# Squares of four RMS norms: from GpSimd to ScalarE and VectorE, and later in the order

## The chip, the core and the metric

The kernel runs on one core of a Trainium2 chip. The metric is the device time of one execution in microseconds, the median of several runs. The engines are TensorE (PE in the profile), VectorE (DVE), ScalarE (ACT), GpSimd (POOL) and SyncE (SP), which issues nearly all DMAs.

## What is computed

Two layers of an encoder trunk on 256 tokens of 1024 features, in float32. Before each of four sublayers stands an RMS norm, and one at the end:

```python
def rms_norm(x, g):
    xf = x.astype(jnp.float32)
    y = xf * lax.rsqrt(jnp.mean(xf * xf, axis=-1, keepdims=True) + RMS_EPS)
    return (y * g.astype(jnp.float32)).astype(x.dtype)
...
    for layer in range(DEPTH):                       # DEPTH = 2
        xn = rms_norm(x, norm_mix[layer])
        if layer % 2 == 0:                           # neighbourhood + latent attention
            x = x + even_mixer(xn, ...)
        else:                                        # dilated sliding windows
            x = x + odd_mixer(xn, ...)
        x = x + sq_relu_mlp(rms_norm(x, norm_mlp[layer]), mlp_w1[layer], mlp_w2[layer])
    return rms_norm(x, norm_final)
```

The change concerns the mean of `xf * xf` in the first four norms.

## The kernel before

The tokens `x` lie transposed in SBUF: 128 partitions of features, eight tiles of features, 256 tokens each. A float32 product runs as three passes on TensorE over operands that are split in two parts of lower precision: high x high, low x high, high x low. The high part is a copy by ScalarE, the low part a subtraction by VectorE. For the weights these are `whi` (L167) and `wlo` (L168), made from `raw`, which SyncE's DMAs fill ahead of time (four buffers of `raw`, three of the split parts). A piece of weights is split in four parts of 128x512 or less. For the tokens they are `xh` (L207, tokens times gain) and `xl` (L208).

The factor 1 / rms is not put onto the tokens. The products take the tokens times the gain, and the factor follows where their results go. So the sum of squares is needed some time after the products begin. Squares of two tiles of features at a time are added into `squares`, 128 x 512, whose halves are added at the end (`add_squares`, L214 to L218). TensorE sums over the partitions by a product with a constant: `columns` (L224) or `inverse_row` (L244). GpSimd takes the power -1/2 (L232, L198).

There are five stages, and the four that the change touches begin like this:

- The start: for each of eight tiles of features `xh`, `xl` and a piece of `w_c` are made, and six products of 416 columns follow (the low-rank inputs of the latent attention). Then come the values of the neighbourhood attention (`v_steps`, products of 512 columns), for two tiles of tokens, in two halves of features each. Here the order on TensorE, ScalarE and VectorE is the order of the code (`manual_schedule`).
- Handovers 1, 2 and 3 (`hand_over`): the last products of a stage end pair by pair; for each pair of tiles VectorE adds the residual (L282, L284), then `xh` and `xl` are made, with a raised priority. Handover 1 leads into the first MLP, 2 into the odd layer, 3 into the last MLP. In an MLP the first piece of `w1` takes 48 products of 256 columns (`up(0)`), in the odd layer the first values take 48 products of 384 columns.

Outside of the manual part a scheduler sets the order on each engine, by priorities and its own estimates. An engine works off its instructions in that order.

Of the kernel before, what the change touches and what calls it, by code (L numbers as in the profile page):

```python
"""Two layers of a hybrid encoder trunk (neighbourhood + latent attention, then dilated
attention, each with a squared-ReLU MLP) on one core.

The float32 products of the projections run as three passes over operands split into two
float32r parts each (12 + 12 bits): high*high + low*high + high*low.
"""
# [12 lines left out]
AF = mybir.ActivationFunctionType  # L19
# [4 lines left out]
P = 128  # L24
D = 1024
KT = D // P
T = 256
# [17 lines left out]
def trunk(ctx, tc, a, out):  # L45
# [9 lines left out]
    def scratch(shape, name):  # L55
        """A rotating [P, 512] float32 tile, seen in another shape."""
        n = int(np.prod(shape))
        v = work.tile([P, 512], F32, tag="scratch", name=name, bufs=12)[:, :n]
        if len(shape) == 2:
            v = v.rearrange("p (a b) -> p a b", b=shape[1])  # L60
        return v
# [12 lines left out]
    # the array's clock rises with work: keep it busy until the first operands are there  # L74
# [21 lines left out]
    # ---------------------------------------------------------------- weights  # L96
# [61 lines left out]
    def weight():  # L158
        """The next piece of the weights, as its two parts; those after it are on their way."""
        j = state["used"]  # L160
        prefetch(j + 1, j + 1)
        prefetch(j + LOAD_AHEAD, j + SPLIT_AHEAD)
        state["used"] = j + 1
        return parts.pop(j)[1:]
# [10 lines left out]
    def two_heads(o, hi, lo, ts):  # L175
        """Scores of two heads, in the two halves of the rows, in turns."""
        for n, (y, z) in enumerate(((hi, hi), (hi, lo), (lo, hi))):
            for j in range(2):
                pb = slice(64 * j, 64 * j + 64)
                nc.tensor.matmul(o[j], y[pb, 0, ts], z[pb, 1, :], start=n == 0, stop=n == 2)  # L180

    def weave(main, side, lead=0):
        """Issue two lists of steps, the second spread evenly over the first from lead on."""
        done = 0
        for i, step in enumerate(main):
            step()
            while done < len(side) and done * (len(main) - lead) < (i + 1 - lead) * len(side):
                side[done]()
                done += 1
# [4 lines left out]
    # ------------------------------------------------------------------ norms  # L194
    # The products take the tokens times the gain alone; 1 / rms follows where their results go.
# [5 lines left out]
    def two(z):  # L201
        return z.rearrange("p (f n) -> p f n", f=2)

    def prepare(k, n, xT):
        """The gain of norm n on a tile of features, and its two parts: steps."""
        hi, lo, gk = xT[0][:, k, :], xT[1][:, k, :], gains[:, n * KT + k:n * KT + k + 1]
        return (lambda: nc.scalar.activation(hi, x[:, k, :], AF.Copy, scale=gk),  # L207
                lambda: nc.vector.scalar_tensor_tensor(lo, x[:, k, :], gk, hi.bitcast(F32), ALU.mult, ALU.subtract))  # L208

    def add_squares(b, s):  # L210
        """Squares of two tiles of features onto their sum; the last leaves one of all."""
        v = x[:, 2 * b:2 * b + 2, :]
        q = scratch([2, T], "q") if b else two(s)
        nc.gpsimd.tensor_tensor(q, v, v, op=ALU.mult)  # L214
        if b:
            nc.gpsimd.tensor_tensor(two(s), two(s), q, op=ALU.add)
        if b == 3:
            nc.gpsimd.tensor_tensor(s[:, 0:T], s[:, 0:T], s[:, T:2 * T], op=ALU.add)  # L218

    def columns(s):  # L220
        """Mean square + EPS of the tokens, as a column for each tile of them."""
        pr = bank("w")
        for t in range(NT):
            nc.tensor.matmul(pr[:, t:t + 1], s[:, tok(t)], mean[:, 0:1], start=True, stop=True)  # L224
        ms = work.tile([P, NT], F32, tag="ms", name="ms")
        nc.vector.tensor_scalar(ms, pr[:, 0:NT], EPS, None, ALU.add)
        return ms

    def rstd(s):
        """1 / rms of the tokens, as columns."""  # L230
        r = work.tile([P, NT], F32, tag="rstd", name="rstd")
        nc.gpsimd.tensor_tensor(r, columns(s), mhalf.broadcast_to([P, NT]), op=ALU.pow)  # L232
        return r

    def inverse_columns(s):
        """1 / mean square of the tokens, as columns."""
        inv = columns(s)
        nc.vector.reciprocal(inv, inv)
        return inv

    def inverse_row(s):
        """1 / mean square of the tokens, as a row that is the same for all partitions."""
# [12 lines left out]
    def as_row(dg):  # L255
        """Columns, given as diagonals, as a row that is the same for all partitions."""
        pr = bank("w")
        for t in range(NT):
            nc.tensor.matmul(pr[:, tok(t)], mean, dg[t], start=True, stop=True)
        return pr[:, 0:T]  # L260
# [11 lines left out]
    def hand_over(accs, last, n, scale=None):  # L272
        """The residual, in pairs of tiles of features, while the products of the next pair run."""
        xT = half_tile(act, "xh", 2), half_tile(act, "xl", 2)
        s = sum_tile()
        for b in range(4):
# [10 lines left out]
            add_squares(b, s)  # L287
# [5 lines left out]
    def onto(accs, w, c, v, m, first, last, fbs):  # L293
        """Products of a tile of features, [feature, token], for some of the eight tiles of sums."""
# [7 lines left out]
    def out_steps(accs, mixed, wo, k):  # L302
        """A tile of features of the output projection, in two steps."""
# [6 lines left out]
    def out_last(accs, mixed, wo):  # L310
        """The last two tiles of features, by pairs of tiles of sums."""
# [7 lines left out]
    def mlp(mp, xT, invert, tail, make_down, beside=lambda j: None):  # L319
        """The first product and the second but for its last pieces of weights: returns what  # L320
        these take."""
        hs = {}

        def up(j):
            w = weight()
            pu = bank("w")
            # the last features of the first piece come later than the others
# [13 lines left out]

        for j in range(3):
            up(j)
        inv = invert()
# [11 lines left out]
    def mlp_between(mp, xT, s):  # L356
# [5 lines left out]
        accs, hs, inv, w = mlp(mp, xT, lambda: inverse_row(s), range(14, 16), down)  # L362
# [8 lines left out]
    def finish(mp, xT, s):  # L371
        """The last MLP and the final norm, [token, feature]."""
# [17 lines left out]
        def tokens_first(j):  # L390
            """Transpose the tokens back, a part at a time."""
# [7 lines left out]
        accs, hs, inv, w = mlp(mp, xT, lambda: inverse_columns(s), tail, down, tokens_first)  # L399
# [22 lines left out]
        # the last tile piece by piece, so that little is left after the last product  # L422
# [22 lines left out]
    # ============================================================== even layer  # L445
    def even(ep):
# [17 lines left out]
        def rope(dst, src, n, cos, sin, half):  # L464
            """dst, src [P, n, 2*half]; cos, sin [P, 2*half], the sine signed."""
# [8 lines left out]
        # low-rank inputs of the latent attention, its shared rotary key, and the  # L474
        # values of the neighbourhood attention
# [53 lines left out]
        with tc.manual_schedule(engines={ENG.PE, ENG.Activation, ENG.DVE}):  # L529
            for k in range(KT):  # L530
# [8 lines left out]
                if k % 2:  # L539
                    add_squares(k // 2, s)  # L540
# [3 lines left out]
        with tc.issue_after(ins[0]), tc.issue_after(ins[1]):  # L544
            with tc.manual_schedule(engines={ENG.PE, ENG.Activation, ENG.DVE}):
                v0, v1 = v_steps(0), v_steps(1)
                v0(range(4))
                small_loads()
                r = rstd(s)
                dg = [diagonal(r, t) for t in range(NT)]  # L550
                v1(range(4))
# [6 lines left out]
        # queries and keys of the neighbourhood attention, [head dim of two heads, token]  # L558
# [21 lines left out]
        # latent attention: queries, keys, values  # L580
# [56 lines left out]
        # both attentions: two heads of one tile of queries at a time, in three steps  # L637
# [10 lines left out]
        def scores(n):  # L648
            kind, t, hp = items[n]
            load_bias(n + 2)  # L650
            # the two heads of the neighbourhood attention lie in different row tiles: a bank each
# [47 lines left out]
        def attention():  # L699
            """Steps for all items, each a step behind the one before, the first with time to go by."""  # L700
# [20 lines left out]
        # the steps of the projections with their time on the tensor engine, and between them,  # L721
        # spread evenly after the first, those of the attention
# [21 lines left out]
    # =============================================================== odd layer  # L744
    def odd(op, xT, s):
# [7 lines left out]
        # keys of the two strided groups of a head, block diagonal for each class of tokens  # L753
# [13 lines left out]
        def value_steps(d):  # L767
            """Steps for the values of two heads in the three groups, [token, feature]."""
# [23 lines left out]
        def qk_steps(d):  # L792
            """Steps for the queries and keys of two heads, [feature, token]: of the first group,
            both heads; then by head those of the other two."""
# [85 lines left out]
        run_all(v0[0::2] + v0[1::2])  # L880
# [40 lines left out]
def _order():  # L921
    """Tokens by class modulo 4, then 16; the strided groups attend within a class."""
# [25 lines left out]
def _layout(i):  # L948
# [10 lines left out]
    # queries and keys of two heads: the first group's, then by head those of the other two  # L959
# [8 lines left out]
    # bias of [query, key], where the key is in the query's window, else a filling  # L968
# [33 lines left out]
```

## Time and profile before

| | |
|---|---|
| Median of 3 runs | 787.64 us (786.34 to 788.21) |
| Span of the profiled execution, first to last instruction | 787.1 us; the profile gives no other time of its own for it |
| TensorE busy | 766.1 us, 97% of the span |
| VectorE, ScalarE, GpSimd busy | 516.8, 500.7, 47.9 us |
| Mean granted TensorE clock | 0.990 |
| DMA | 129.14 MB, mean 164 GB/s |

A row of a timeline gives the start, the duration, the engine, the line, the operation with the tiles it writes and reads, how many such instructions are merged into it, and in brackets the engine's idle time ahead of it with what ended it. Matmuls overlap: a product lasts 0.28 us in the record while the next starts 0.12 us after it, so a pace is read from starts. A row of a window gives the stretch and its length, the busy time of each engine, the granted clock and the DMA share.

### The profile page before, as it was taken

How to read it: one execution, taken by the hardware profiler on the slowest of the kernel's cores; microseconds unless marked ns; L12 is line 12 of the kernel's file. 1: busy time of each engine (PE TensorE's matmuls, PEld its weight loads, DVE VectorE, ACT ScalarE, POOL GpSimd, SP SyncE). 2: the span in 40 equal slices, each digit the busy share in tenths (PEclk: the TensorE clock that was granted, in tenths of full speed). 3: DMA queues.
4: the chain of work that ended last, by engine and by line, in shares of the span. 5: the costliest groups of instructions: out<-in, count | busy, mean ns of one | idle time of the engine just before them, and what ended most of it. 6: DMA issues, size and time to landing. Idle time of an engine off the chain costs nothing. (4 is left out here: it accounts for less than half of the span.)

```text
span 787.1 us, 14625 instructions
## 1 busy us (share of the span) xinstructions
PE 766.1 (97%) x5898; PEld 723.9 (92%) x5898; DVE 516.8 (66%) x1012; ACT 500.7 (64%) x1062; POOL 47.9 (6%) x54
## 2 busy tenths in 40 slices
PE   7999998999999999899999999999998999999996
PEld 5898898999999999799999999999997999999996
DVE  7778859665555548777676767676749555546554
ACT  6578964444545444588989889889854545545451
POOL 5100004000000002300000000000004000000000
PEclk9999999999999999899999999999999999999999
DMA  8754223544545544444535434535453544555511
GB/s 297 271 202 149 108 107 107 202 174 163 212 167 185 184 168 162 161 138 144 174 126 183 149 134 162 166 117 200 147 197 114 214 164 172 199 184 191 166 50 53
DMA packets 22819, 129.14 MB, mean 164 GB/s; under 512 B 2912, under 2 KB 5472, under 8 KB 9824
## 3 DMA queue, kind: packets, MB, share of 16 engines
q1 hardware_dynamic: 22464, 127.94, 46.2%
q8 instruction: 46, 0.75, 0.4%
q10 hardware_dynamic: 288, 0.28, 0.1%
q14 instruction: 21, 0.17, 0.1%
HBM read 127.16 MB, written 1.05 MB: 163 GB/s over the span
## 5 line engine op out<-in xcount | busy, mean ns | idle before, releaser
L168 DVE TENSOR_TENSOR wlo<-raw,whi 128x512 fp32r<-128x512 f32 (+3 forms) x488 | 314.0, 677 | 165.8 <-ACT whi L167 164.8
L167 ACT CAST whi<-raw 128x512 fp32r<-128x512 f32 (+3 forms) x488 | 268.9, 600 | 220.4 <-issue 178.0
L172 PE MATMUL w<-xl,whi 128*128 128x256 f32 x528 | 150.9, 286 | 5.8 <-DVE xl L208 5.8
L173 PE MATMUL w<-xh,wlo 128*128 128x256 f32 x528 | 149.6, 283 | 0.0
L171 PE MATMUL w<-xh,whi 128*128 128x256 f32 x528 | 149.4, 283 | 0.0
L171 PE MATMUL acc<-xh,whi 128*128 128x256 f32 x432 | 125.3, 290 | 0.0
L173 PE MATMUL acc<-xh,wlo 128*128 128x256 f32 x432 | 121.8, 282 | 0.0
L172 PE MATMUL acc<-xl,whi 128*128 128x256 f32 x432 | 121.7, 282 | 0.0
L172 PEld LDWEIGHTS w<-xl,whi 128*128 128x128 f32 x528 | 99.9, 189 | 8.0 <-DVE xl L208 7.5
L171 PEld LDWEIGHTS w<-xh,whi 128*128 128x128 f32 x528 | 100.4, 190 | 0.5
L173 PEld LDWEIGHTS w<-xh,wlo 128*128 128x128 f32 x528 | 100.3, 190 | 0.0
L171 PEld LDWEIGHTS acc<-xh,whi 128*128 128x128 f32 x432 | 81.4, 188 | 2.4 <-issue 1.4
L172 PEld LDWEIGHTS acc<-xl,whi 128*128 128x128 f32 x432 | 81.5, 189 | 0.0
L173 PEld LDWEIGHTS acc<-xh,wlo 128*128 128x128 f32 x432 | 81.2, 188 | 0.0
L171 PE MATMUL acc<-hh,whi 128*128 128x256 f32 x256 | 72.6, 284 | 0.0
L172 PE MATMUL acc<-hl,whi 128*128 128x256 f32 x256 | 72.4, 283 | 0.0
L173 PE MATMUL acc<-hh,wlo 128*128 128x256 f32 x256 | 72.4, 283 | 0.0
L172 PE MATMUL acc<-wlo,xh 128*128 128x384 f32 (+2 forms) x160 | 57.7, 360 | 3.3 <-DVE wlo L168 3.3
L173 PE MATMUL acc<-whi,xl 128*128 128x384 f32 (+2 forms) x160 | 57.4, 359 | 3.2 <-DVE xl L208 3.2
L171 PE MATMUL acc<-whi,xh 128*128 128x384 f32 (+2 forms) x160 | 59.6, 372 | 0.4 <-ACT xh L207 0.4
L171 PEld LDWEIGHTS acc<-hh,whi 128*128 128x128 f32 x256 | 49.1, 192 | 0.0
L173 PEld LDWEIGHTS acc<-hh,wlo 128*128 128x128 f32 x256 | 49.1, 192 | 0.0
(202 smaller groups left out, 1332.4 us busy)
## 6 DMA issues: line engine op xcount, KB each, us to landing
raw<-in_w SPq DMA_DIRECT2D x64, 1024.0 KB, 4.8
raw<-in_w_oqk SPq DMA_DIRECT2D x24, 1024.0 KB, 4.8
raw<-in_w_ov SPq DMA_DIRECT2D x16, 768.0 KB, 4.3
raw<-in_w_qk SPq DMA_DIRECT2D x4, 1024.0 KB, 10.3
raw<-in_w_oe SPq DMA_DIRECT2D x4, 1024.0 KB, 5.1
raw<-in_w_oo SPq DMA_DIRECT2D x4, 1024.0 KB, 4.8
bias<-in_rpb SPq DMA_DIRECT2D x8, 256.0 KB, 3.8
raw<-in_w_c SPq DMA_DIRECT2D x8, 208.0 KB, 4.6
```

What stands on the lines that cost most here:

```text
L167: a = nc.scalar.copy(hi, src).ins
L168: return a, (eng or nc.vector).tensor_tensor(lo, src, hi.bitcast(F32), op=ALU.subtract).ins
L171: nc.tensor.matmul(o, sh, mh, start=first, stop=False)
L172: nc.tensor.matmul(o, sh, ml, start=False, stop=False)
L173: nc.tensor.matmul(o, sl, mh, start=False, stop=last)
```

## The change

`add_squares` goes. `square_steps` gives four steps in its place, in which ScalarE squares and VectorE adds. They are called at other points: at the start once all `w_c` and the first half of `w_v` are split, ahead of `v0(range(4))`, with `rstd` (the product with `mean`, then the power) moved behind `v1(range(4))`; in both MLPs two steps after each of `up(1)` and `up(2)`; in the odd layer between the four steps of the first values, from the second on.

```diff
-    def add_squares(b, s):
-        v = x[:, 2 * b:2 * b + 2, :]
-        q = scratch([2, T], "q") if b else two(s)
-        nc.gpsimd.tensor_tensor(q, v, v, op=ALU.mult)
-        if b:
-            nc.gpsimd.tensor_tensor(two(s), two(s), q, op=ALU.add)
-        if b == 3:
-            nc.gpsimd.tensor_tensor(s[:, 0:T], s[:, 0:T], s[:, T:2 * T], op=ALU.add)
+    def square_steps(s):
+        def square(b):
+            q = scratch([2, T], "q") if b else two(s)
+            nc.scalar.activation(q, x[:, 2 * b:2 * b + 2, :], AF.Square)
+            if b:
+                nc.vector.tensor_tensor(two(s), two(s), q, op=ALU.add)
+            if b == 3:
+                nc.vector.tensor_tensor(s[:, 0:T], s[:, 0:T], s[:, T:2 * T], op=ALU.add)
+        return [lambda b=b: square(b) for b in range(4)]
...
     def hand_over(accs, last, n, scale=None):
...
-            add_squares(b, s)
...
+        squares = square_steps(s)
         for j in range(3):
             up(j)
+            run_all(squares[2 * j - 2:2 * j])
         inv = invert()
...
     def even(ep):
...
-                if k % 2:
-                    add_squares(k // 2, s)
...
                 v0, v1 = v_steps(0), v_steps(1)
+                run_all(square_steps(s))
                 v0(range(4))
                 small_loads()
+                v1(range(4))
                 r = rstd(s)
                 dg = [diagonal(r, t) for t in range(NT)]
-                v1(range(4))
...
     def odd(op, xT, s):
...
-        run_all(v0[0::2] + v0[1::2])
+        squares = square_steps(s)
+        weave(v0[0::2] + v0[1::2], squares, 1)
         r = [rstd(s)]
```

All DMAs keep their order. Behind the changed lines the line numbers rise by one or two.

The order on VectorE at the start, before, from the last two tokens' low parts (`xl`) on:

```order
L208 SCALAR_TENSOR_TENSOR xl<-x,gains,xh 128x256
L168 TENSOR_TENSOR wlo<-raw,whi 128x416
L208 SCALAR_TENSOR_TENSOR xl<-x,gains,xh 128x256
L168 TENSOR_TENSOR wlo<-raw,whi 128x416
L168 TENSOR_TENSOR wlo<-raw,whi 128x512 x8
L226 TENSOR_SCALAR ms<-w 128x2
```

And there now:

```order
L208 SCALAR_TENSOR_TENSOR xl<-x,gains,xh 128x256
L168 TENSOR_TENSOR wlo<-raw,whi 128x416
L168 TENSOR_TENSOR wlo<-raw,whi 128x512 x4
L216 TENSOR_TENSOR squares<-squares,q 128x512 x3
L218 TENSOR_TENSOR squares<-squares 128x256
L168 TENSOR_TENSOR wlo<-raw,whi 128x512 x4
L227 TENSOR_SCALAR ms<-w 128x2
```

The four additions stand between the two halves of `w_v` (`wlo` of 128x512).

The order on VectorE at the odd layer's head, before, from the residual of the last pair of tiles on (128x384 are the odd layer's first weights, 128x512 the queries' and keys'):

```order
L284 TENSOR_TENSOR x<-scaled,x 128x512
L168 TENSOR_TENSOR wlo<-raw,whi 128x384 x2
L168 TENSOR_TENSOR wlo<-raw,whi 128x512
L208 SCALAR_TENSOR_TENSOR xl<-x,gains,xh 128x256 x2
L168 TENSOR_TENSOR wlo<-raw,whi 128x512 x7
L226 TENSOR_SCALAR ms<-w 128x2
```

And there now:

```order
L285 TENSOR_TENSOR x<-scaled,x 128x512
L168 TENSOR_TENSOR wlo<-raw,whi 128x384 x2
L216 TENSOR_TENSOR squares<-squares,q 128x512
L208 SCALAR_TENSOR_TENSOR xl<-x,gains,xh 128x256 x2
L168 TENSOR_TENSOR wlo<-raw,whi 128x512 x4
L216 TENSOR_TENSOR squares<-squares,q 128x512
L168 TENSOR_TENSOR wlo<-raw,whi 128x512
L216 TENSOR_TENSOR squares<-squares,q 128x512
L168 TENSOR_TENSOR wlo<-raw,whi 128x512
L218 TENSOR_TENSOR squares<-squares 128x256
L168 TENSOR_TENSOR wlo<-raw,whi 128x512
L227 TENSOR_SCALAR ms<-w 128x2
```

One addition comes ahead of the last pair's `xl`, the others among the pieces of weights behind it. On TensorE the product with `squares` (L224, now L225) stood right behind the 48 products of the values. It now stands eleven products further, among those of the queries, and thirteen ahead of the product with the diagonals (L259, now L260).

More of the change, by code (lines that the diff above doesn't have):

```diff
@@ L317, in out_last, with mlp @@
         return [lambda b=b: step(b) for b in range(4)]
-    def mlp(mp, xT, invert, tail, make_down, beside=lambda j: None):
+    def mlp(mp, xT, s, invert, tail, make_down, beside=lambda j: None):
         hs = {}
@@ L360, in down @@
             return step
-        accs, hs, inv, w = mlp(mp, xT, lambda: inverse_row(s), range(14, 16), down)
+        accs, hs, inv, w = mlp(mp, xT, s, lambda: inverse_row(s), range(14, 16), down)
         def last(b):
@@ L397, in tokens_first @@
                 nc.scalar.copy(xt[:, t, HALF[h]], pt)
-        accs, hs, inv, w = mlp(mp, xT, lambda: inverse_columns(s), tail, down, tokens_first)
+        accs, hs, inv, w = mlp(mp, xT, s, lambda: inverse_columns(s), tail, down, tokens_first)
         jf = [(j, f) for j in w for f in range(2)]
```

## The prediction

> **What bounds the kernel now.** I read the page first, for the busy shares, then the list of waits for TensorE (who waited for whom: total us, times, longest), then the timelines of the four places where those waits lie.
>
> ```profile
> PE 766.1 (97%) x5898; PEld 723.9 (92%) x5898; DVE 516.8 (66%) x1012; ACT 500.7 (64%) x1062; POOL 47.9 (6%) x54
> PE w L172 <- DVE xl L208: 5.8, 7, 1.7
> PE acc L172 <- DVE wlo L168: 3.3, 4, 1.4
> PE acc L173 <- DVE xl L208: 3.2, 1, 3.2
> ```
>
> TensorE is busy for 97% of the span, so only what it waits for can be won, and what a lowered clock costs it. The three rows of waits make 12.3 us, all of it waits for VectorE at the heads of the four stages: the low parts `xl` of the tokens, and in the first stage the low parts `wlo` of the weights. The timeline tells why VectorE is late there (start, duration, engine, line):
>
> ```profile
> 4.28 0.48 DVE L208 SCALAR_TENSOR_TENSOR xl<-x,gains,xh 128x256 fp32r<-128x256 f32 x1 [3.15 <-ACT xh L207]
> 13.46 1.50 DVE L208 SCALAR_TENSOR_TENSOR xl<-x,gains,xh 128x256 fp32r<-128x256 f32 x1
> 18.70 0.47 DVE L208 SCALAR_TENSOR_TENSOR xl<-x,gains,xh 128x256 fp32r<-128x256 f32 x1
> 11.63 3.06 POOL L216 TENSOR_TENSOR squares<-squares,q 128x512 f32<-128x512 f32 x2
> 17.53 0.79 POOL L218 TENSOR_TENSOR squares<-squares 128x256 f32<-128x256 f32 x1
> 118.69 1.28 DVE L284 TENSOR_TENSOR x<-acc,x 128x512 f32<-128x512 f32 x2
> 119.52 1.04 POOL L214 TENSOR_TENSOR squares<-x 128x512 f32<-128x512 f32 x1 [43.31 <-DVE x L284]
> L208 DVE SCALAR_TENSOR_TENSOR xl<-x,gains,xh 128x256 fp32r<-128x256 f32 x32 | 31.6, 1027 | 4.7 <-ACT xh L207 4.6
> ```
>
> The same `xl` takes 0.47 us while GpSimd is idle (at 4.28, and at 18.70 just after its last addition) and 1.50 us beside GpSimd's additions; over all 32 the mean is 1027 ns. The additions of L284, which take one operand from PSUM, run at 0.64 us each beside a GpSimd square. So VectorE instructions with two operands in SBUF are held up while GpSimd works on the squares. 0.40 us of `xl` after another is what I count without it (0.47 less the overlap of neighbours), 0.6 us for a piece of `wlo`.
>
> **The change, place by place.** All 32 square instructions leave GpSimd. For each place I take TensorE's time from its first product to its next stage, and replace it by the count of products times their pace at full clock; then I ask whether the operands come in time.
>
> Handover 1 (into the first MLP): three rows of TensorE, then a window of 5 us (behind its length the busy us of TensorE, its weight loads, VectorE, ScalarE and GpSimd, then granted clock, DMA share and GB/s), then the preparation:
>
> ```profile
> 121.88 0.29 PE L171 MATMUL w<-xh,whi 128*128 128x256 f32 x1
> 127.65 0.38 PE L172 MATMUL w<-xl,whi 128*128 128x256 f32 x1 [1.70 <-DVE xl L208]
> 132.86 0.28 PE L171 MATMUL w<-xh,whi 128*128 128x256 f32 x1
> 132.98 0.28 PE L172 MATMUL w<-xl,whi 128*128 128x256 f32 x1
> 130.00:135.00 5.00, 5.00 (x33) 5.00 (x33) 4.28 (x8) 2.06 (x5) 0.78 (x1) 0.73 0.18 39
> 119.41 1.71 ACT L207 ACTIVATE xh<-x,gains 128x256 fp32r<-128x256 f32 x4 [1.64 <-DVE x L284]
> 119.95 3.90 DVE L208 SCALAR_TENSOR_TENSOR xl<-x,gains,xh 128x256 fp32r<-128x256 f32 x4
> 121.96 1.14 ACT L167 CAST whi<-raw 128x512 fp32r<-128x512 f32 x2 [0.84 <-PE acc L172]
> ```
>
> From 121.88 to 132.86 stand the 48 products of the first piece of w1. Their pace is 0.12 us (132.86 to 132.98), so 5.75 us would do and 10.98 were taken: 5.2 us, of which (1 - 0.73) x 5 = 1.4 are the lowered clock after the waits. Without the holds the first four `xl` take 4 x 0.4 instead of 3.90 us and end near 121.6. The last four follow ScalarE's `xh`, which come 0.43 us apart (1.71 / 4) behind the two casts that end at 123.1; so they end at 124.0 to 125.2, and TensorE at full pace asks for them at 124.8 to 126.5. Gain 5.2 us. ScalarE's one early Square there falls into the 0.84 us in which it waited for TensorE.
>
> Handover 3 (into the last MLP) is the same code:
>
> ```profile
> 594.40 0.28 PE L171 MATMUL w<-xh,whi 128*128 128x256 f32 x1
> 604.43 0.29 PE L171 MATMUL w<-xh,whi 128*128 128x256 f32 x1
> 600.00:605.00 5.00, 4.10 (x28) 3.48 (x29) 5.00 (x6) 0.45 (x1) 2.88 (x3) 1.00 0.48 192
> ```
>
> 10.03 us less 5.75 is 4.3 us; the clock did not fall here. The Square that ScalarE now runs between two pairs of `xh` costs 0.6 us there, and `xl` still ends 0.5 us or more ahead of TensorE.
>
> Handover 2 (into the odd layer):
>
> ```profile
> 311.75 0.34 PE L171 MATMUL acc<-whi,xh 128*128 128x384 f32 x1
> 313.31 0.34 PE L171 MATMUL acc<-whi,xh 128*128 128x384 f32 x1
> 321.28 0.69 PE L173 MATMUL acc<-whi,xl 128*128 128x384 f32 x1 [3.16 <-DVE xl L208]
> 326.57 0.82 PE L224 MATMUL w<-mean,squares 128*128 128x1 f32 x4
> 320.00:325.00 5.00, 3.72 (x12) 3.72 (x13) 5.00 (x9) 0.44 (x1) 0.94 (x1) 0.54 0.57 210
> 327.66 0.71 POOL L232 TENSOR_TENSOR rstd<-ms,mhalf 128x2 f32<-128x2 f32 x1 [6.72 <-DVE ms L226]
> ```
>
> 48 products of values, nine of them in 1.56 us (311.75 to 313.31): 8.3 us would do, 14.8 were taken, so 6.5 us. Against it stands a new wait. The first addition of squares is queued straight ahead of the last two `xl` (+0.65 us; they then end near 316.9, TensorE asks at 317.3), and the last one behind four pieces of `wlo`, two more additions and two more pieces: 316.9 + 4 x 0.6 + 0.65 + 0.6 + 0.65 + 0.6 + 0.4 = 322.2. TensorE's product with `squares` now stands 11 products into the queries, at 320.1 + 1.3 = 321.4, and everything of TensorE is queued behind it: 0.8 us. Then VectorE, GpSimd's power (0.71 us) and the diagonals have only 13 products (1.6 us) until L260 needs them, some 0.2 us too few. Net 6.5 - 1.0 = 5.5 us.
>
> The start:
>
> ```profile
> 9.11 0.55 PE L171 MATMUL acc<-whi,xh 128*128 128x416 f32 x1
> 9.45 0.51 PE L172 MATMUL acc<-wlo,xh 128*128 128x416 f32 x1
> 20.98 0.35 PE L171 MATMUL acc<-whi,xh 128*128 128x416 f32 x1
> 21.54 0.39 PE L171 MATMUL acc<-whi,xh 128*128 128x512 f32 x1
> 13.73 0.54 ACT L167 CAST whi<-raw 128x416 fp32r<-128x416 f32 x1 [0.92 <-DMA raw<-in_w_c]
> 15.02 2.43 ACT L167 CAST whi<-raw 128x512 fp32r<-128x512 f32 x4 [0.74 <-DMA raw<-in_w_v]
> 15.00:20.00 5.00, 3.43 (x9) 2.76 (x10) 5.00 (x6) 3.41 (x7) 3.17 (x3) 0.66 0.93 390
> ```
>
> Here DMA sets a floor: its share is 0.93 in this window, and the last cast of `w_c` waited for its data until 13.73, the first of `w_v` until 15.02. Without the holds VectorE follows ScalarE by one piece, and the last `wlo` of `w_c` ends at 14.9. TensorE, at 0.34 us a product until 9.45 (9.11 to 9.45) and 0.19 after it (three from 20.98 to 21.54) as now, does six products for each of the eight tiles of features and reaches the values at 16.4 in place of 21.54, when their first piece is split (15.02 + 0.6 + 0.65 = 16.3): 5.1 us. The squares then fill ScalarE from 17.5 to 19.8 and VectorE to 20.9, ahead of the second half of `w_v`; its first `wlo` ends at 21.5, TensorE asks after eight groups of 0.7 us, at 22.4. The norm's chain (L225, L198, `cn`) starts only behind v1's first half:
>
> ```profile
> 37.79 0.35 DVE L496 SCALAR_TENSOR_TENSOR cn<-acc,rstd,gc 128x128 f32<-128x128 f32 x1
> 41.18 0.49 PE L504 MATMUL w<-ident,cn 128*128 128x128 f32 x3
> ```
>
> The second `cn` has 3 us in hand before, and TensorE comes 5.1 us earlier while the chain gains only 1.5: 0.5 us of wait. Net 4.6 us.
>
> The work added, 16 Squares on ScalarE, 12 additions and 4 half-size ones on VectorE, is not in the trace under these engines. Near rows:
>
> ```profile
> 773.50 0.63 ACT L409 ACTIVATE junk<-xt 128x512 f32<-128x512 f32 x1
> L168 DVE TENSOR_TENSOR hl<-hsq,hh 128x512 fp32r<-128x512 f32 x32 | 21.9, 684 | 0.0
> ```
>
> 16 x 0.63 = 10 us and 12 x 0.68 + 4 x 0.42 = 9.9 us. In both MLPs they are covered: a piece of weights is split a whole product (5.75 us) ahead, and 0.68 us at a time uses that up nowhere. The cover ends where VectorE is full, at the odd layer's head, counted above. Bounds: nothing (added work can win none), or all 2.3 us of VectorE's additions once for each of the three handovers (7 us). I take the 1.0 us worked out for the odd layer's head, the nearest row being the window from 320 on, where VectorE is busy for all 5 us.
>
> Sum: 4.6 + 5.2 + 5.5 + 4.3 = 19.6 us; 787.1 - 19.6 = 767.5 us of span. The runs' median, 787.64, is 0.5 us above the span, so 768.0.
>
> **The rivals.**
> (a) The start stays bound by DMA and by the squares put ahead of the second half of `w_v`. For it: DMA share 0.93 and both casts that wait for data. Against it: those casts begin at 13.7 and 15.0 while TensorE finished at 21.5. With 0.5 us gained there instead of 4.6: 772.1. It decides if `w_v`'s second half is split later than 22.4.
> (b) The lowered clock stays. The slow stretches after waits (by the three windows with a low clock 1.4 us in handover 1, (1 - 0.54) x 5 = 2.3 in handover 2, (1 - 0.66) x 5 = 1.7 at the start) would then be no consequence of them: 768.0 + 5.4 = 773.4. For it: handover 3 had the same 2.9 us of waits and kept clock 1.00, so waits do not suffice. Against it: all three windows lie right behind waits. The Trainium skill, "TensorE: Matmul & The Clock Gate", HAM oscillation, asks for no idle gaps over about 3.4 us, and every gap here is shorter; by that rule this rival is the forecast. The trace disagrees: behind gaps of 1.70 and 3.16 us at most, the clock stood at 0.73 and 0.54.
> (c) The squares come late at the odd layer's head by 3.5 us instead of 1: 770.5. For it: VectorE had no idle time there in 320 to 325.
> (d) Slower. VectorE's holds are not GpSimd's but come from ScalarE's reads beside it; then they stay, `xl` keeps 1.0 to 1.5 us, nothing of the 19.6 is won, and the addition ahead of the last `xl` in handover 2 (1.3 us at that rate) and the late `squares` behind it (another 0.9) are lost: 789.8. It decides if `xl` stays above 1 us with GpSimd idle. Against it: 0.47 us at 18.70, beside ScalarE's casts.
> (e) The order puts squares beside the preparation after all: one Square and one addition in each handover at most, so it is inside the sum.
>
> **How the numbers follow.** Forecast (with (e) in it; 765.5 to 770) 0.62; (a) 0.13; (b) 0.08; (c) 0.09; (d) 0.03; several of (a) to (c) together, above 774, 0.05, of which 0.02 end within 0.2%, about what a measurement of this kernel can tell from no change. Upwards the range takes in (a), (b) and (c), and 768.0 with 7 us of additions in place of 1.0, 774. Downwards it goes to 5.1 + 5.2 + 6.5 + 4.3 = 21.1 us with no new wait, 766.5, less the 1.3 us by which the lowest run lies under the median: 765. Faster by over 0.2% is all but (d) and those 0.02: 0.95; within 0.02; slower 0.03.
>
> **What would show it.** GpSimd busy near 9 us instead of 47.9; mean of `xl` under 500 ns; TensorE's waits for `xl` and `wlo` from 12.3 to under 2 us; `acc` 128x512 (values) first at about 16.4; the first piece of w1 done in about 5.8 us after both handovers; no window behind a handover with a clock under 0.9. New and small: a wait of L225 for `squares` at the odd head. It is wrong if `xl` stays long, if waits for `squares` or `whi` take the place of those gone, or if the low clock windows remain.

## Result and the profile after

| | before | after |
|---|---|---|
| Median | 786.99 us (785.76 to 788.21, 4 runs) | 769.33 us (769.10 to 769.99, 4 runs) |
| Span of the profiled execution | 787.1 us | 767.5 us |
| Mean granted clock there | 0.990 | 0.999 |

The ratio is 0.9769 (95% interval 0.9752 to 0.9786): the changed kernel is 2.3% faster, 17.7 us by the medians. One execution of the variant below that has only the handovers early ran at a granted clock of 0.753 and took 908.66 us; no ratio uses it.

The page's busy times:

```profile
PE 757.4 (99%) x5898; PEld 716.9 (93%) x5898; DVE 501.7 (65%) x1028; ACT 508.0 (66%) x1078; POOL 9.9 (1%) x22
```

TensorE's whole list of waits (total us, times, longest):

```profile
PE acc L81 <- DVE warm L76: 1.2, 1, 1.2
PE acc L171 <- ACT whi L167: 0.9, 1, 0.9
PE w L858 <- ACT pp L851: 0.8, 1, 0.8
PE w L506 <- DVE cn L498: 0.5, 1, 0.5
PE acc L172 <- DVE wlo L168: 0.4, 2, 0.2
```

The group of `xl` (busy us, mean ns of one):

```profile
L208 DVE SCALAR_TENSOR_TENSOR xl<-x,gains,xh 128x256 fp32r<-128x256 f32 x32 | 14.1, 481 | 4.4 <-ACT xh L207 4.3
```

Of the 12.3 us of waits for `xl` and `wlo` 0.4 us are left. The 32 `xl` take 481 ns each in place of 1027, though VectorE now has 16 additions more: it is busy for 501.7 us, 15 us less than before, because it is no longer held.

The places, in timelines: the first and the 17th L171 product of the first MLP (48 products apart), the same in the last MLP, the odd layer's head, and the values at the start.

```profile
117.67 0.29 PE L171 MATMUL w<-xh,whi 128*128 128x256 f32 x1
123.42 0.29 PE L171 MATMUL w<-xh,whi 128*128 128x256 f32 x1
578.95 0.29 PE L171 MATMUL w<-xh,whi 128*128 128x256 f32 x1
584.71 0.29 PE L171 MATMUL w<-xh,whi 128*128 128x256 f32 x1
311.81 0.42 DVE L218 TENSOR_TENSOR squares<-squares 128x256 f32<-128x256 f32 x1
312.29 0.61 PE L225 MATMUL w<-mean,squares 128*128 128x1 f32 x4
314.62 0.71 PE L260 MATMUL w<-diag,mean 128*128 128x128 f32 x4
16.00 0.50 PE L171 MATMUL acc<-whi,xh 128*128 128x512 f32 x1
```

From 117.67 to 123.42 are 5.75 us and from 578.95 to 584.71 are 5.76: the 48 products at full pace. The windows behind the handovers, and two at the start, show the clock (next to last the DMA share):

```profile
10.00:15.00 5.00, 5.00 (x29) 4.98 (x28) 3.72 (x8) 2.99 (x7) 0.00 (x0) 1.00 1.00 311
15.00:20.00 5.00, 4.78 (x21) 3.58 (x20) 3.63 (x6) 4.53 (x9) 0.00 (x0) 1.00 1.01 424
125.00:130.00 5.00, 5.00 (x44) 5.00 (x43) 2.89 (x6) 2.38 (x6) 0.00 (x0) 1.00 0.58 210
320.00:325.00 5.00, 5.00 (x44) 5.00 (x43) 3.81 (x7) 4.07 (x8) 0.00 (x0) 1.00 0.36 140
```

No window behind a handover has a clock under 1.00 (0.73 and 0.54 before). With the starts of the stages in both traces the 19.6 us of span are made up as follows:

| stretch | before | after | gained |
|---|---|---|---|
| span's start to the first value product | 21.54 | 16.00 | 5.54 |
| from there to the first product of w1 | 100.34 | 101.67 | -1.33 |
| first piece of w1 (handover 1) | 10.98 | 5.75 | 5.23 |
| from there to the odd layer's values | 178.89 | 179.08 | -0.19 |
| values to queries (handover 2) | 15.50 | 8.32 | 7.18 |
| queries to the last MLP | 267.15 | 268.13 | -0.98 |
| its first piece of w1 (handover 3) | 10.03 | 5.76 | 4.27 |
| from there to the end | 182.7 | 182.8 | -0.1 |

The 7.18 us of handover 2 hold 0.68 us that only moved: the four products with `squares` lay ahead of the queries (326.57 to 327.25) and lie behind their start now, in the next line of the table. They were slow there, at the lowered clock; at full clock the four take 0.36 us (310.07 to 310.43 in the variant with the squares early).

### The profile page after: what moved, and what is told of

It is laid out like the page before. It is cut to its first block, busy times and chain, and to the rows that moved or that the text cites. A ratio compares the mean times of both kernels' runs of the same rounds, so it can differ in the third digit from the quotient of the medians.

```text
span 767.5 us, 14613 instructions
## 1 busy us (share of the span) xinstructions
PE 757.4 (99%) x5898; PEld 716.9 (93%) x5898; DVE 501.7 (65%) x1028; ACT 508.0 (66%) x1078; POOL 9.9 (1%) x22
## 4 chain that ended last, share of the span: by engine, by line
PE 87%; ACT 5%; DVE 4%; issue 2%; DMA 2%; POOL 1%; SPq 0%; POOLq 0%; DVEq 0%
PE acc L171 18%; PE acc L172 18%; PE acc L173 18%; PE w L171 8%; PE w L172 8%; PE w L173 8%; DVE wlo L168 2%; PE w L180 1%; ACT whi L167 1%; PE w L858 1%; PE w L682 1%; PE w L842 1%; DMA raw<-in_w_v 1%; PE w L696 1%; PE acc L867 1%
## 5 line engine op out<-in xcount | busy, mean ns | idle before, releaser
L168 DVE TENSOR_TENSOR wlo<-raw,whi 128x512 fp32r<-128x512 f32 (+3 forms) x488 | 307.9, 664 | 169.6 <-ACT whi L167 168.7
L172 PE MATMUL w<-xl,whi 128*128 128x256 f32 x528 | 149.1, 282 | 0.0
L171 PE MATMUL w<-xh,whi 128*128 128x256 f32 x528 | 148.9, 282 | 0.0
L171 PE MATMUL acc<-xh,whi 128*128 128x256 f32 x432 | 125.2, 290 | 0.0
L171 PEld LDWEIGHTS w<-xh,whi 128*128 128x128 f32 x528 | 99.6, 189 | 0.5
L171 PEld LDWEIGHTS acc<-xh,whi 128*128 128x128 f32 x432 | 81.4, 188 | 2.4 <-issue 1.4
L171 PE MATMUL acc<-hh,whi 128*128 128x256 f32 x256 | 72.6, 284 | 0.0
L171 PE MATMUL acc<-whi,xh 128*128 128x384 f32 (+2 forms) x160 | 57.6, 360 | 0.9 <-ACT whi L167 0.9
L172 PE MATMUL acc<-wlo,xh 128*128 128x384 f32 (+2 forms) x160 | 55.3, 346 | 0.4 <-DVE wlo L168 0.4
L173 PE MATMUL acc<-whi,xl 128*128 128x384 f32 (+2 forms) x160 | 55.0, 344 | 0.0
L171 PEld LDWEIGHTS acc<-hh,whi 128*128 128x128 f32 x256 | 49.1, 192 | 0.0
## 6 DMA issues: line engine op xcount, KB each, us to landing
raw<-in_w_ov SPq DMA_DIRECT2D x16, 768.0 KB, 4.2
```

The source lines that it names most:

```text
L168: return a, (eng or nc.vector).tensor_tensor(lo, src, hi.bitcast(F32), op=ALU.subtract).ins
L171: nc.tensor.matmul(o, sh, mh, start=first, stop=False)
L172: nc.tensor.matmul(o, sh, ml, start=False, stop=False)
L173: nc.tensor.matmul(o, sl, mh, start=False, stop=last)
```

## Experiments

Four questions: is it GpSimd's work or the place of the squares that matters; what in GpSimd's work holds VectorE; do the later places gain anything; and does the clock fall by the waits. In the diffs a minus is the changed kernel, unless something else is said; `...` stands for lines left out.

**Late, but on GpSimd.**

```diff
 def square(b):
     q = scratch([2, T], "q") if b else two(s)
-    nc.scalar.activation(q, x[:, 2 * b:2 * b + 2, :], AF.Square)
+    nc.gpsimd.tensor_tensor(q, x[:, 2 * b:2 * b + 2, :], x[:, 2 * b:2 * b + 2, :], op=ALU.mult)
     if b:
-        nc.vector.tensor_tensor(two(s), two(s), q, op=ALU.add)
+        nc.gpsimd.tensor_tensor(two(s), two(s), q, op=ALU.add)
...
```

(The last addition, of the halves, goes to GpSimd as well.)

> The changed kernel with the squares and additions given back to GpSimd, issued at the new, later points of the code. Theory (GpSimd instructions that read SBUF hold up VectorE's instructions with two SBUF operands): GpSimd has nothing else to do, so in the handovers it starts each square as soon as its tokens are there, whatever the point in the code; xl is held as before there (mean of xl 0.8 to 1.0 us), only the start may gain its 4 us: 778 to 788 us. Rival (the place in the order is what counts, not the engine): 768 to 771 us.

Measured: 787.68 us, ratio to before 1.0003 (0.9990 to 1.0016). The group of `xl`, and the head of TensorE's list of waits:

```profile
L208 DVE SCALAR_TENSOR_TENSOR xl<-x,gains,xh 128x256 fp32r<-128x256 f32 x32 | 29.0, 946 | 4.2 <-ACT xh L207 4.2
```

```profile
PE w L172 <- DVE xl L208: 5.7, 7, 1.5
PE acc L172 <- DVE wlo L168: 4.6, 6, 1.6
PE acc L173 <- DVE xl L208: 4.0, 1, 4.0
```

With GpSimd kept, the later places in the program win nothing: GpSimd gets to its squares when the tokens are there, so they still lie beside the preparation. At the start too the values begin at 21.14 us, 0.4 us ahead of before, and not at 16.00.

**Early, on ScalarE and VectorE.** The code of before, with only `add_squares` changed.

```diff
-    nc.gpsimd.tensor_tensor(q, v, v, op=ALU.mult)
+    nc.scalar.activation(q, v, AF.Square)
     if b:
-        nc.gpsimd.tensor_tensor(two(s), two(s), q, op=ALU.add)
+        nc.vector.tensor_tensor(two(s), two(s), q, op=ALU.add)
```

(Here the minus is the kernel before; the last addition, of the halves, goes to VectorE as well.)

> The kernel before with its squares by ScalarE and its additions by VectorE, left at the old points beside the preparation. Theory: nearly all is won, since xl is not held (mean 0.48 us); up to 0.65 us for each addition that is queued ahead of an xl, at most 1 to 5 us in all: 769 to 774 us. Rival (the later place counts): 784 to 788 us.

Measured: 767.90 us (767.54 to 768.21), ratio 0.9748 (0.9732 to 0.9763), span 766.0: 1.4 us faster than the changed kernel. TensorE's whole list of waits:

```profile
PE acc L81 <- DVE warm L76: 1.2, 1, 1.2
PE w L857 <- ACT pp L850: 0.8, 1, 0.8
PE acc L172 <- DVE wlo L168: 0.2, 1, 0.2
```

So the whole gain comes from the engines, and the later places take 1.4 us of it back. The two ratios' intervals overlap; the executions do not (767.54 to 768.21 us, against 769.10 to 769.99).

**No squares at all.**

```diff
-        v = x[:, 2 * b:2 * b + 2, :]
-        q = scratch([2, T], "q") if b else two(s)
-        nc.gpsimd.tensor_tensor(q, v, v, op=ALU.mult)
...
+        if b == 0:
+            nc.gpsimd.memset(s, 1.0)
```

(Here the minus is the kernel before. All of `add_squares` is left out but for one constant for each norm, so this kernel leaves out the four norms.)

> The kernel before with no squares at all: the sums are filled with a constant once per norm, so four norms are not computed. It bounds what any arrangement of the squares can give. Theory: no hold and none of the new work, so the changed kernel's remaining waits for squares and cn (0.2 + 0.3 + 0.5 us) are all that is left to win: 767 to 769.5 us. Rival (the squares on ScalarE and VectorE still cost several us in the MLPs and the odd layer): 762 to 766 us.

Measured: 767.77 us (767.51 to 768.87), span 766.1. Without the work it is no faster than the variant before this one with all of it: 9.7 us on ScalarE and 9.9 us on VectorE cost nothing. By this run another arrangement of the squares could win some 1.6 us over the changed kernel (767.77 against 769.33), and the variant before has nearly all of it.

**The changed kernel, with GpSimd reading beside it.** Results that nobody reads, at the 16 old places:

```diff
+    def beside(b):
+        v, w = x[:, 2 * b:2 * b + 2, :], warm.rearrange("p (f n) -> p f n", f=2)
+        nc.gpsimd.tensor_tensor(w, v, v, op=ALU.mult)
...
```

> The changed kernel, and in addition 32 GpSimd instructions of the old kind (two operands from the tokens in SBUF) at the old points; nobody reads their results. Theory: the hold alone makes the time: mean of xl back near 1.0 us, TensorE's waits for xl and wlo near 12 us, 785 to 790 us. Rival (the order of the squares, or the shorter dependence through squares, made the gain): 769 to 771 us.

Measured: 785.91 us, ratio 0.9973 (0.9960 to 0.9986). The groups of GpSimd's products and of `xl`, then the rows for `xl`, `wlo` and `squares` in TensorE's list of waits, then two windows behind handover 1:

```profile
L223 POOL TENSOR_TENSOR warm<-x 128x512 bf16<-128x512 f32 x16 | 17.9, 1117 | 491.5 <-DVE x L293 485.8 <-PE acc L81 3.4 <-DMA x<-in_x 1.8
L208 DVE SCALAR_TENSOR_TENSOR xl<-x,gains,xh 128x256 fp32r<-128x256 f32 x32 | 29.8, 968 | 4.4 <-ACT xh L207 4.2
```

```profile
PE w L172 <- DVE xl L208: 4.7, 6, 1.5
PE acc L172 <- DVE wlo L168: 3.9, 5, 1.1
PE acc L173 <- DVE xl L208: 2.9, 1, 2.9
PE w L233 <- DVE squares L218: 1.2, 1, 1.2
```

```profile
120.00:125.00 5.00, 3.78 (x30) 3.36 (x28) 5.00 (x7) 3.55 (x9) 3.42 (x4) 1.00 0.26 111
125.00:130.00 5.00, 3.58 (x24) 3.13 (x25) 5.00 (x7) 0.43 (x2) 3.27 (x4) 1.00 0.00 0
```

Nothing waits for GpSimd's results here, and 16.6 us of the gain are gone (785.91 against 769.33). The waits for `xl` and `wlo`, 11.5 us, are nearly those of the kernel before (12.3). So its loss was the hold, not that `squares` came late.

**GpSimd that copies, and GpSimd that only writes.** In place of the products above, copies (`nc.gpsimd.tensor_copy(w, v)`; 60 of them by the profile, where the expectation says 28) or 120 memsets. The diff is that of the memsets:

```diff
+        nc.gpsimd.tensor_copy(w[:, :, 0:1], v[:, :, 0:1])
+        for _ in range(4 * (1 + (b > 0)) + 2 * (b == 3)):
+            nc.gpsimd.memset(warm, 0.0)
```

> The changed kernel, with GpSimd copies of x into an unread bf16 tile at the 16 old places (28 copies of 128x512: one operand read in place of two). Theory (one read of SBUF is enough for a hold): xl above 700 ns, TensorE waits for xl or wlo for 6 us or more, 778 to 788 us (each copy perhaps shorter than the 1.04 us of the squares, so some of the loss may be missing). Rival (only GpSimd instructions with two operands hold VectorE): xl under 520 ns, 768 to 771 us.

> The changed kernel, with GpSimd doing something else at the 16 old places: a one-column copy of x (so that it starts when the old squares started) and then 4, 8, 8 and 10 memsets of a 128x512 bf16 tile that nothing reads, in place of the squares; GpSimd writes SBUF and reads nearly nothing. Theory (VectorE's two-operand instructions are held by GpSimd's reads of SBUF): the mean of xl stays under 520 ns, TensorE's waits for xl and wlo under 1 us together, time 769.3 within 0.2% (768 to 771). Rival (any GpSimd instruction at work holds VectorE): xl above 800 ns and 780 to 790 us. The Trainium skill, 'SBUF — State Buffer', Who interferes with whom, says that an instruction that only writes does not contend with VectorE's second input: by it 769.3.

Measured: copies 778.73 us, ratio 0.9883 (0.9857 to 0.9908); memsets 775.99 us, ratio 0.9856 (0.9833 to 0.9878). First the copies' own group and their group of `xl`, then the memsets' group of `xl`:

```profile
L224 POOL CAST warm<-x 128x512 bf16<-128x512 f32 x60 | 46.1, 768 | 485.9 <-DVE x L290 477.5
L208 DVE SCALAR_TENSOR_TENSOR xl<-x,gains,xh 128x256 fp32r<-128x256 f32 x32 | 23.4, 770 | 4.3 <-ACT xh L207 4.2
```

```profile
L208 DVE SCALAR_TENSOR_TENSOR xl<-x,gains,xh 128x256 fp32r<-128x256 f32 x32 | 14.1, 481 | 5.1 <-ACT xh L207 5.0
```

One operand read is enough for a hold. That the mean is lower (770 ns against 968) goes with the shorter instructions, 768 ns a copy against 1117 a product; the last section shows row by row that the hold is the same. The copies' time is as the first theory expected, its waits are not: TensorE waits 3.1 us for `xl` and `wlo`, not 6, and another 2.5 for `squares`, whose additions come late behind the held instructions; at the start the values begin 2.8 us later than in the changed kernel (18.77). Beside memsets `xl` is at 481 ns, as with GpSimd idle: no hold. This is what the Trainium skill says ("SBUF — State Buffer", Who interferes with whom): a VectorE instruction with two SBUF inputs contends with a GpSimd instruction that reads SBUF, not with one that only writes; these three means agree. But the memsets' time, 776, missed both theories. TensorE's longest wait, the timeline of GpSimd at the odd layer's head, and the windows there show why:

```profile
PE w L266 <- DVE diag L259: 4.2, 1, 4.2
```

```profile
312.66 4.60 POOL L225 MEMSET warm<- 128x512 bf16 x8
317.23 0.69 POOL L239 TENSOR_TENSOR rstd<-ms,mhalf 128x2 f32<-128x2 f32 x1
```

```profile
315.00:320.00 5.00, 1.48 (x7) 1.48 (x8) 1.31 (x5) 1.08 (x3) 3.77 (x7) 0.79 0.47 193
320.00:325.00 5.00, 5.00 (x38) 5.00 (x38) 3.63 (x7) 3.43 (x8) 0.00 (x0) 0.86 0.20 43
```

The norm's power (317.23) stood in GpSimd's queue behind eight memsets, the diagonals behind it, and TensorE behind those for 4.2 us; after it the clock was 0.79 and 0.86. I had costed the memsets by what they do to VectorE and not by the queue they stand in.

**Writes, with the queue clear.** The memsets of the last two pairs in that handover left out:

```diff
-            beside(b)
+            if n != 2 or b < 2:
+                beside(b)
```

(Here the minus is the kernel with the memsets.)

> The kernel with GpSimd's memsets at the old places, without those after the last two pairs of tiles of the handover into the odd layer: there they stood in GpSimd's queue ahead of the norm's power, and TensorE waited 4.25 us for the diagonals. Theory (the 6.7 us by which that kernel was slower than the changed one are this queue, the clock that is lowered behind the wait, and nothing of them is a hold of VectorE): the wait for diag is under 0.3 us, xl stays at 0.48 us, handovers 1 and 3 take 5.8 us with GpSimd busy, time 769.5 (768.5 to 771). Rival (writes of GpSimd also slow something else by 1 us or more): 771 to 776 with the wait for diag gone.

Measured: 769.30 us (768.97 to 769.40), ratio 0.9763 (0.9742 to 0.9784), with GpSimd busy for 67 us. The mean of `xl` is 481 ns, the wait for `diag` is gone from TensorE's list, and the first pieces of w1 take 5.76 us after both handovers. The window behind handover 1:

```profile
120.00:125.00 5.00, 5.00 (x44) 5.00 (x43) 3.67 (x7) 3.03 (x7) 4.47 (x10) 1.00 0.27 69
```

GpSimd works for 4.47 of 5 us here, TensorE for all 5 at full clock. GpSimd may be busy with memsets beside the preparation; and its activity does not lower the clock here.

**Half early.** Where the later places cost the 1.4 us: only the first norm early (with its columns), or only the three handovers.

```diff
 # only the first norm early, with its columns
+        steps = square_steps(s)
...
+                if k % 2:
+                    steps[k // 2]()
...
-                run_all(square_steps(s))
...
-                v1(range(4))
                 r = rstd(s)
                 dg = [diagonal(r, t) for t in range(NT)]
+                v1(range(4))
```

```diff
 # only the handovers early
+        steps = square_steps(s)
...
+            steps[b]()
         return xT, s
...
-        squares = square_steps(s)
...
-            run_all(squares[2 * j - 2:2 * j])
...
-        squares = square_steps(s)
-        weave(v0[0::2] + v0[1::2], squares, 1)
+        run_all(v0[0::2] + v0[1::2])
```

> The changed kernel, with the squares of the first norm (and its columns) back at the old places, by ScalarE and VectorE; the other three norms stay late. The variant with all four early was 1.4 us faster than the changed kernel; by the two traces it was ahead by 0.57 us at handover 1. Theory (the late start costs TensorE the 0.48 us of the wait for the second cn, because the norm's columns now stand behind v1's first half): that wait is gone, the first product of w1 stands at 117.1 instead of 117.67, time 768.7 (768.2 to 769.1). Rival (the 1.4 us come from the handovers alone): 769.3 and the first product of w1 at 117.6.

> The changed kernel, with the squares of the three handovers at the old places, by ScalarE and VectorE, and those of the first norm late. It is the other half of the variant with all four early. Theory: the handovers' share of the 1.4 us is 0.9 (by the two traces 0.18 from the first product of w1 to the values of the odd layer, 0.62 from there to the last MLP, 0.12 behind it): 768.4 (767.9 to 768.9), the wait for squares at the odd layer's head gone, the wait for cn still 0.5. Rival (early squares push xh or wlo back in a handover, and the start alone made the gain): 769.3 or more, with new waits for xl or wlo in TensorE's list.

Measured: 768.49 us (ratio 0.9758, 0.9739 to 0.9777) and 768.37 us (0.9756, 0.9738 to 0.9775). The two gains, 0.84 and 0.96 us, add up to 1.8; both together had given 1.4. With the start early the wait for `cn` is gone from TensorE's list and the first product of w1 stands at 116.63, earlier than the 117.1 expected. With the handovers early the list ends with

```profile
PE acc L172 <- DVE wlo L168: 0.7, 4, 0.2
PE w L506 <- DVE cn L498: 0.5, 1, 0.5
```

`cn` is still there, as expected, and `wlo` has 0.3 us more than in the changed kernel, a little of what the rival said. Both theories held in time. Differences this small rest on the single executions (768.17 to 769.02 and 768.32 to 768.65 us, against 769.10 to 769.99) more than on the ratios, whose intervals overlap.

**Smaller loads of w_v**, on top of the variant with all four early:

```diff
-        load_weight(2)
-        load_weight()
+        load_weight(4)
+        load_weight(2)
```

(Here the minus is that variant.)

> The variant with all four norms' squares early on ScalarE and VectorE, with w_v's two loads cut into 4 and 2 pieces in place of 2 and 1, so that the first of its splits need not wait for 512 KB. By the trace of that variant TensorE waits there 0.23 us for wlo and the first two value products take 0.5 us more than the others. Theory: up to 0.6 us of it goes, 767.3 (766.9 to 768.0). Rival (SyncE's three more issues at 0.43 us each delay what comes behind by as much): 767.9 or more.

Measured: 767.51 us (767.28 to 767.75), ratio 0.9742 (0.9721 to 0.9763), span 765.3: the fastest of all, but its runs overlap those of the variant without it, and the 0.2 us of wait for `wlo` that it was to remove is still in the list. That it helps is not shown: its values take 11.93 us to the next stage where that variant's take 12.30, but so they do in the one with only the first norm early, whose loads are uncut.

## Why the prediction was right, point by point

768.0 us were forecast (765.5 to 770) and 769.33 measured; the span was forecast at 767.5 and is 767.5. That the span agrees to 0.1 us is luck: handover 2 gave 0.7 us more than forecast, the start 0.4 less, and 0.3 of loss had been forgotten. The mechanism is not luck; it stands on four runs: hold back with reads of GpSimd (785.91), back with the squares on GpSimd at the late places (787.68), gone with them on the other engines at the old places (767.90), absent beside writes (769.30).

- **The time around the span was mis-sized.** The forecast added 0.5 us; in each of the four runs of the changed kernel the time is 1.9 us above that run's span. The step that went wrong is the comparison of one profiled span with a median of other executions: in 36 executions of the kernel before the time is 1.8 us above the span too, but the spans go from 783.7 us at a mean clock of 0.996 to 788.5 at 0.988. The profiled one, 787.1 at 0.990, was longer than most. So 19.6 us of span were won against that execution, and 17.7 to 18.6 us against the medians (786.99 and 787.9).
- **Handovers 1 and 3: exact.** 5.23 and 4.27 us, against 5.2 and 4.3.
- **Handover 2: 6.2 instead of 5.5 us** (7.18 less 0.98). The 6.5 us from the operands were right: the 48 products went from 14.82 us to 8.32. The four products with `squares` got 0.3 us shorter by the clock, and the new waits cost 0.6 us and not 1.0. The order on VectorE was the one counted through; but the last `xl` ended 4.57 us behind the first value product (302.50 to 307.07 in the timeline) and not 5.15, so `squares` was there at 312.23, and TensorE lost some 0.25 us on it and not 0.8. At the diagonals it lost 0.3 us where 0.2 was forecast (the product due at 314.39 came at 315.09, and the four with the diagonals take 0.36): GpSimd's power took 1.07 us instead of 0.71, for a reason that the last section gives.
- **The start: 4.2 instead of 4.6 us** (5.54 less 1.33). The values began at 16.00 where 16.4 was forecast, by a step that was wrong in its parts: TensorE's products were at full pace (0.19 us) from 5.67 on, not from 9.45, and the time won so was spent waiting for the data of `w_c`, in rows of the timeline of ScalarE and TensorE:

```profile
6.85 0.54 ACT L167 CAST whi<-raw 128x416 fp32r<-128x416 f32 x1 [1.57 <-DMA raw<-in_w_c]
7.44 0.46 PE L171 MATMUL acc<-whi,xh 128*128 128x416 f32 x1 [0.87 <-ACT whi L167]
15.33 2.42 ACT L167 CAST whi<-raw 128x512 fp32r<-128x512 f32 x4 [1.69 <-DMA raw<-in_w_v]
```

From 10 to 20 us the DMA share is 1.00, and at these points the start waits for transfers, which rival (a) had seen; between them TensorE is busy at full pace (5.00 of 5 us from 10 to 15). In all eight runs in which GpSimd reads no tokens, or one column of them, the values begin at 15.67 to 16.26, wherever the squares stand or without any. The forecast's test of rival (a) has a slip: 16.4 and eight groups of 0.7 us make 22.0, not 22.4. The first `wlo` of `w_v`'s second half was there at 22.19 (21.50 and 0.69), and the first product that needs it began at 22.89.

The wait for the second `cn` came as forecast (0.48 us); for the other 0.85 us nothing had been put in. 0.58 of it went within the values, which now wait for `w_v` (12.26 us from their first product to the next stage, 11.68 before; 0.23 us is a wait for `wlo`). The last 0.27 us stands between there and the first product of w1; with the first norm early that stretch is as before (88.72 us, 88.66 before, 89.41 in the changed kernel).
- **Forgotten:** 0.2 us in the first MLP and 0.1 us in the last.
- **Rival (b), a clock that stays low, is out.** In the windows of the changed kernel, and beside memsets with the queue clear, the clock behind the handovers is 1.00, and a wait that has nothing to do with the preparation (4.2 us for `diag`) brought 0.79 and 0.86. (The rival's price left out a fourth window, 325 to 330 in the kernel before, at 0.78: 1.1 us more.) Not every wait does: in the two windows of the kernel with GpSimd's unread products TensorE was idle for 2.6 of ten us, at a clock of 1.00, while in the same run the clock was 0.66 behind handover 3 (595 to 600), where the kernel before kept 1.00. What decides it stays open; the spread of the kernel before (785.5 to 790.3 us, against 769.1 to 770.0) goes with the clock. The Trainium skill's bound of some 3.4 us of idle time ("TensorE: Matmul & The Clock Gate", HAM oscillation) fits the 4.2 us wait, and not the 0.73 that was seen behind waits of 1.70 us at most.
- **Rivals (a) and (c) are out in their size:** the start gained 4.2 us and not 0.5, and the wait for `squares` cost some 0.25 us at the odd layer's head and not 3.5.
- **Rival (d), holds by ScalarE's reads, is out:** with ScalarE squaring beside the preparation (the variant with all four early) `xl` takes 480 ns.

## What to carry to other kernels

Before moving work in time, ask which engine it is on: VectorE instructions with two operands in SBUF are held by GpSimd's products and copies out of SBUF until the one in progress ends (its memsets did not hold them), and while the squares stayed on GpSimd a later place in the code changed nothing. Work of 10 us on each of two engines that are two thirds busy was free in all four places, even right beside the critical preparation; issued later than needed it cost 1.4 us, part of it in waits of what depends on it. And compare a profiled span with the spans of the other runs, not with their times, before taking a median as the base.

## What was not expected of the hardware

- VectorE stands until the GpSimd instruction in progress has ended. Three rows of the kernel before, at the start:

```profile
10.19 0.58 DVE L168 TENSOR_TENSOR wlo<-raw,whi 128x416 fp32r<-128x416 f32 x1
10.21 1.46 POOL L214 TENSOR_TENSOR q<-x 128x512 f32<-128x512 f32 x1 [0.79 <-DMA x<-in_x]
10.69 1.26 DVE L208 SCALAR_TENSOR_TENSOR xl<-x,gains,xh 128x256 fp32r<-128x256 f32 x1
```

`wlo` started first and kept its 0.58 us, and the square behind it took 1.46 us where one that nothing holds takes 1.04 (119.52 in the same trace, in the prediction's rows). `xl` started while the square ran and ended at 11.95, 0.28 us behind it (11.67). The same 0.28 us, within 0.04, follows each of GpSimd's additions, unread products and copies into which an `xl` started, at the start of the kernel before and of three variants, and in handover 1 of two of these. An example beside copies: one of 8.96 to 9.81, and the `xl` of 9.26 ends at 10.09. So a copy holds VectorE no less than a product does; it is over sooner. The Trainium skill states it so ("SBUF — State Buffer", SBUF: two separate sides): whichever of the two starts first has the shared ports for the whole instruction, and the other is fully blocked. These rows agree.
- The same hold slows GpSimd. Its power on 128x2 takes 0.71 us where VectorE is idle beside it (327.66 in the kernel before) and 1.07 where a `wlo` had started ahead of it: at the odd layer's head of the changed kernel the power starts at 313.17, the `wlo` of 0.68 us at 313.01.
- An operand in PSUM makes the difference that the forecast took from the additions at 118.69, where GpSimd's square began only 0.45 us before they ended. A better row is in the trace of the copies: the addition of 121.06, with one operand in PSUM, starts while a copy runs (120.93 to 121.62) and takes 0.68 us, as the one behind it that starts beside none.
- At the start TensorE's clock rises at different times with the same warm-up ahead. In the timeline of the changed kernel the pace is 0.19 us from the fourth product on, in that of the early variant 0.35 until 6.82 and 0.19 from 7.11; the values began at 16.00 and 16.11 all the same, since the first cast of `w_v` had its data only at 15.33 and 15.44.

```profile
5.85 0.35 PE L171 MATMUL acc<-whi,xh 128*128 128x416 f32 x1
6.04 0.35 PE L172 MATMUL acc<-wlo,xh 128*128 128x416 f32 x1
```

```profile
6.47 0.55 PE L172 MATMUL acc<-wlo,xh 128*128 128x416 f32 x1
6.82 0.45 PE L173 MATMUL acc<-whi,xl 128*128 128x416 f32 x1
7.11 0.35 PE L171 MATMUL acc<-whi,xh 128*128 128x416 f32 x1
7.30 0.42 PE L172 MATMUL acc<-wlo,xh 128*128 128x416 f32 x1
```
